# Issuing the sums and normalising of one attention step ahead of the next step's scores

## The chip, the cores and the metric

The kernel runs on one core of a Trainium2 chip. The metric is the device time of one execution in microseconds (us). Before the change it is 1518.8 us, the median of 3 runs (1518.49 to 1519.86). A core has five engines that work side by side, each on its own queue of instructions in order: TensorE (PE: matrix products and transposes), VectorE (DVE), ScalarE (ACT), GpSimd (POOL) and SyncE (SP), which issues most DMAs. An instruction that has to wait holds up everything behind it on its engine.

## The reference

One step of a two-layer network over 384 tokens of width 1024: 128 context tokens and 256 latent tokens. Each layer is SwiGLU, a mixer, SwiGLU, each behind a norm with a shift, a scale and a gate. The mixer of layer 0 ("even") is differential attention with 4 heads beside a short convolution; that of layer 1 ("odd") is attention with 16 query heads, 4 key heads, a window and a sink logit. Context tokens see only context tokens.

```python
# even: two softmaxes per head, subtracted; one query block (128 rows) at a time
s = jnp.einsum("bqhmd,bkhmd->bhmqk", qi, k) * scale
p = jax.nn.softmax(s, axis=-1)
a = p[:, :, 0] - lam * p[:, :, 1]
o = jnp.einsum("bhqk,bkhe->bqhe", a, v)
# odd: one softmax over context keys, latent keys in the window, and a sink
s_l = jnp.where(valid, s_l, -jnp.inf)
p = jax.nn.softmax(jnp.concatenate([s_c, s_l, sink_column], axis=-1), axis=-1)
o = (jnp.einsum("bgrqc,bcgd->bqgrd", p[..., :p_len], v_ctx)
     + jnp.einsum("bgrqk,bkgd->bqgrd", p[..., p_len:-1], vs))
```

## The kernel before

The 384 tokens lie along the free dimension, so a weight block of 128 by 128 meets 384 columns at once. Float32 products are made of three matmuls on split operands (`mm3`, L178 to L180): every weight unit of 1024 x 256 is split into a high part (`wh`, ACT, L80) and a low part (`wl`, L84, in two halves: DVE, and in the mixers GpSimd for the second). `refill` or `refill_half` does the next split at the end of each step of a pipeline. Instructions are issued in the order in which the Python code runs; no scheduler reorders them.

Attention is cut into steps and run by `pipeline`. A step has four parts, of which those of several steps interleave:

- `a`, the scores: PE makes the scores of two maps in two PSUM tiles (`s`), DVE takes their maxima (`mx` L961, `omx` L1221), multiplies by the scale and negates (`ng` L963; `omx` L1223, `ong` L1225, `oes` L1229), ACT takes the exponentials with their row sums (L971; L1233, and L1237 for the sink's term `oes`).
- `m`, the sums, reciprocals and normalising. Even (`combined`): DVE alone, L980 to L992. Odd (`normalised`): an add L1241 and a reciprocal L1242 on two columns on DVE, then one multiply of both maps on GpSimd (L1243).
- `b`, the transposes on PE (`aT`) and their copies by ACT into `at_sb` (L1008, L1255).
- `c`, the products with the values on PE (`o` L1022, `oo` L1266), and at the end of a group of steps what follows it (even: squares, sums and `on`; odd: the split of `oo` into `gh` by ACT L1273 and `gl` by DVE L1274).

At the pipeline's step s, `a` is that of attention step s, `m` that of s-1, `b` that of s-lag and `c` that of s-lag-1. Between `m` and `b` stands `fill`, which gives PE other work: even, the convolution's projections (`conv_chunks`, with their own work on DVE and ACT); odd, pieces of the projections of later queries with their rotary embedding (`rope`, four DVE operations), and near the end the first products of the output projection.

Even has 9 steps and lag 2: step 0 has eight maps of 128 keys for the context tokens, steps 1 to 8 have two maps of 384 keys. Odd has 24 steps and lag 3: every third step (0, 3, 6, ...) is of 128 keys, the others of 384. The scores use the PSUM tag "at" and the transposes "mm", four tiles each, shared with other users.

Of the kernel before, what the change touches and what calls it, by code (L numbers as in the profile page):

```python
# [58 lines left out]
class Weights:  # L59
# [82 lines left out]
    def refill(self):  # L142
        self.split(self.np + self.SPLIT)
# [10 lines left out]
class Kernel:  # L154
# [637 lines left out]
    def pipeline(self, n, a, m, b, c, lag, fill, refill):  # L792

        for s in range(n + lag + 1):
            if s < n:
                a(s)
            if 0 <= s - 1 < n:
                m(s - 1)
            fill(s)
            if 0 <= s - lag < n:  # L800
                b(s - lag)
            if 0 <= s - lag - 1 < n:
                c(s - lag - 1)
            refill()
# [832 lines left out]
```

## Time and profile before

| | |
|---|---|
| median of 3 runs | 1518.8 us |
| the profiled execution's own time | 1518.26 us |
| its span, first to last instruction | 1516.5 us |
| PE busy | 1480.2 us, 98% of the span |
| DVE busy | 1065.0 us, 70% |
| ACT busy | 654.8 us, 43% |
| POOL busy | 147.6 us, 10% |
| chain that ended last: PE, DVE, ACT | 86%, 7%, 2% |
| even attention pipeline | about 383 to 455 us after the span's start |
| odd attention pipeline | about 1106 to 1203 us |

Busy time of an engine counts its instructions, not its waits. The chain that ended last follows the last instruction back to what released it, step by step; a share of PE in it says that PE's own queue set the time there. In the two attention stages an instruction's start, read beside the end of what it needs, says who was late.

### The profile page before, as it was taken

How to read it: one execution, taken by the hardware profiler on the slowest of the kernel's cores; microseconds unless marked ns; L12 is line 12 of the kernel's file. 1: busy time of each engine (PE TensorE's matmuls, PEld its weight loads, DVE VectorE, ACT ScalarE, POOL GpSimd, SP SyncE). 2: the span in 40 equal slices, each digit the busy share in tenths (PEclk: the TensorE clock that was granted, in tenths of full speed). 3: DMA queues.
4: the chain of work that ended last, by engine and by line, in shares of the span. 5: the costliest groups of instructions: out<-in, count | busy, mean ns of one | idle time of the engine just before them, and what ended most of it. 6: DMA issues, size and time to landing. Idle time of an engine off the chain costs nothing.

```text
span 1516.5 us, 22716 instructions
## 1 busy us (share of the span) xinstructions
PE 1480.2 (98%) x9082; PEld 1414.6 (93%) x9082; DVE 1065.0 (70%) x1702; ACT 654.8 (43%) x1203; POOL 147.6 (10%) x99
## 2 busy tenths in 40 slices
PE   6999999999999999999999999999998999999998
PEld 6899999999899999999999999999965799999998
DVE  3848898787777887797779868876786485434442
ACT  4632333465555543233454333324666564223331
POOL 0100000015322100000010000000454220000000
PEclk9999999999999999999999999999998999999999
DMA  9848687633323476676536656743230034433421
GB/s 348 280 155 278 202 262 246 215 117 112 108 88 116 144 232 209 202 237 213 187 105 222 223 180 214 245 165 126 86 100 29 5 112 145 134 117 127 139 91 42
DMA packets 191899, 248.61 MB, mean 164 GB/s; under 512 B 5589, under 2 KB 170034, under 8 KB 191794
## 3 DMA queue, kind: packets, MB, share of 16 engines
q1 hardware_dynamic: 190718, 245.79, 49.1%
q8 instruction: 71, 1.16, 0.3%
q10 hardware_dynamic: 1076, 1.38, 0.3%
q14 instruction: 34, 0.28, 0.1%
HBM read 244.26 MB, written 2.36 MB: 163 GB/s over the span
## 4 chain that ended last, share of the span: by engine, by line
PE 86%; DVE 7%; ACT 2%; issue 2%; POOL 1%; DMA 1%; SPq 0%; ACTq 0%; POOLq 0%; DVEq 0%
PE proj L178 18%; PE proj L180 18%; PE proj L179 18%; PE down L178 9%; PE down L179 9%; PE down L180 8%; DVE wl L84 1%; PE m_sum L237 1%; PE oo L1266 1%; DVE acc L342 1%; PE s L1208 1%; PE aT L1253 1%; DMA wm<-in_w_mod 1%; DVE x L347 1%; ACT wh L80 1%
## 5 line engine op out<-in xcount | busy, mean ns | idle before, releaser
L178 PE MATMUL proj<-xh,wh 128*128 128x384 f32 (+1 forms) x1648 | 563.1, 342 | 3.6 <-ACT bias L518 1.8
L180 PE MATMUL proj<-xh,wl 128*128 128x384 f32 (+1 forms) x1648 | 557.3, 338 | 1.1 <-DVE wl L84 1.1
L179 PE MATMUL proj<-xl,wh 128*128 128x384 f32 (+1 forms) x1648 | 556.3, 338 | 0.0
L84 DVE TENSOR_TENSOR wl<-raw,wh 128x1024 fp32r<-128x1024 f32 (+1 forms) x300 | 357.1, 1229 | 148.6 <-ACT wh L80 148.1
L80 ACT ACTIVATE wh<-raw 128x1024 fp32r<-128x1024 f32 x324 | 317.0, 1027 | 152.7 <-PE down L179 79.7
L178 PEld LDWEIGHTS proj<-xh,wh 128*128 128x128 f32 x1648 | 310.5, 188 | 18.2 <-issue 8.5
L180 PEld LDWEIGHTS proj<-xh,wl 128*128 128x128 f32 x1648 | 311.1, 189 | 1.4 <-DVE wl L84 1.4
L179 PEld LDWEIGHTS proj<-xl,wh 128*128 128x128 f32 x1648 | 310.6, 188 | 0.0
L178 PE MATMUL down<-gh,wh 128*128 128x384 f32 x832 | 280.3, 337 | 0.6 <-ACT gh L634 0.6
L179 PE MATMUL down<-gl,wh 128*128 128x384 f32 x832 | 278.8, 335 | 1.3 <-DVE gl L635 1.3
L180 PE MATMUL down<-gh,wl 128*128 128x384 f32 x832 | 278.3, 334 | 0.0
L225 DVE SCALAR_TENSOR_TENSOR macc<-wm,cpad,macc 128x1024 f32<-128x1024 f32 x210 | 259.1, 1279 | 0.1
L178 PEld LDWEIGHTS down<-gh,wh 128*128 128x128 f32 x832 | 156.3, 188 | 3.4 <-issue 2.3
L179 PEld LDWEIGHTS down<-gl,wh 128*128 128x128 f32 x832 | 156.4, 188 | 2.9 <-DVE gl L635 2.6
L180 PEld LDWEIGHTS down<-gh,wl 128*128 128x128 f32 x832 | 156.3, 188 | 0.0
L634 ACT ACTIVATE gh<-gf 128x768 fp32r<-128x768 f32 x44 | 37.2, 846 | 269.9 <-DVE gf L624 265.4
L347 DVE SCALAR_TENSOR_TENSOR x<-down,m,x 128x128 f32<-128x128 f32 x224 | 82.5, 411 | 72.5 <-PE down L180 72.5
L617 ACT ACTIVATE sg<-proj 128x384 f32<-128x384 f32 x78 | 37.9, 490 | 157.9 <-PE proj L180 157.7
L624 DVE TENSOR_TENSOR gf<-proj,sg 128x384 f32<-128x384 f32 x78 | 43.3, 555 | 79.4 <-PE proj L180 79.4
L84 POOL TENSOR_TENSOR wl<-raw,wh 128x1024 fp32r<-128x1024 f32 x24 | 61.3, 2558 | 107.3 <-ACT wh L80 95.4
L635 DVE TENSOR_TENSOR gl<-gf,gh 128x768 fp32r<-128x768 f32 x44 | 42.2, 959 | 40.1 <-ACT gh L634 40.1
L189 POOL TENSOR_TENSOR nr<-nv,neghalf 128x3 f32<-128x3 f32 x6 | 5.1, 852 | 570.6 <-DVE nv L415 570.6
(221 smaller groups left out, 1083.5 us busy)
## 6 DMA issues: line engine op xcount, KB each, us to landing
raw<-in_ffn_w SPq DMA_DIRECT2D x117, 1024.0 KB
wm<-in_w_mod SPq DMA_DIRECT2D x126, 512.0 KB
raw<-in_ffn_w SPq DMA_DIRECT2D x16, 768.0 KB
raw<-in_even_w_in SPq DMA_DIRECT2D x12, 1024.0 KB
raw<-in_odd_w_in SPq DMA_DIRECT2D x6, 1024.0 KB
raw<-in_even_w_out SPq DMA_DIRECT2D x4, 1024.0 KB
raw<-in_odd_w_out SPq DMA_DIRECT2D x4, 1024.0 KB
raw<-in_ffn_w SPq DMA_DIRECT2D x6, 512.0 KB
```

The lines of the kernel that those rows point to most:

```text
L80: self.k.nc.scalar.activation(parts[0][:, a:b], raw[:, a:b], AF.Copy)
L84: engine.tensor_tensor(out=lo[:, a:b], in0=raw[:, a:b], in1=h[:, a:b].bitcast(F32), op=ALU.subtract)
L178: mm(out, w[0], x[0], start=first, stop=False)
L179: mm(out, w[0], x[1], start=False, stop=False)
L180: mm(out, w[1], x[0], start=False, stop=last)
L225: nc.vector.scalar_tensor_tensor(out=acc, in0=t, scalar=c, in1=acc, op0=ALU.mult, op1=ALU.add)
L237: self.nc.tensor.matmul(ps[32 * j:32 * j + 32, 0:256], c, v[:, j], start=first, stop=last)
L347: self.nc.vector.scalar_tensor_tensor(out=self.x[oc][:, a:b], in0=psum[:, a:b], scalar=gate[:, oc, g:g + 1], in1=self.x[oc][:, a:b], op0=A ...
L617: nc.scalar.activation(sg[c], out[:, 0:T], AF.Silu)
L624: nc.vector.tensor_tensor(out=gf[:, c], in0=out[:, 0:T], in1=sg[c], op=ALU.mult)
L634: nc.scalar.activation(gh[:, at:at + 2], gf, AF.Copy)
L635: nc.vector.tensor_tensor(out=gl[:, at:at + 2], in0=gf, in1=gh[:, at:at + 2].bitcast(F32), op=ALU.subtract)
```

## The change

In `pipeline`, `m(s - 1)` is called ahead of `a(s)` and no longer behind it. Nothing else differs.

```diff
     def pipeline(self, n, a, m, b, c, lag, fill, refill):
 
         for s in range(n + lag + 1):
+            if 0 <= s - 1 < n:
+                m(s - 1)
             if s < n:
                 a(s)
-            if 0 <= s - 1 < n:
-                m(s - 1)
             fill(s)
```

The order of instructions changes on DVE alone; on PE, ACT, POOL and SP it is the same as before. The first place is DVE in the even pipeline, from the maxima of step 0 to those of step 1 (`s` scores, `mx` maxima, `ng` their negated scaled values, `rs` row sums, `c_` the second map's factor, `e` the exponentials):

```order
 L955 TENSOR_REDUCE mx<-s 128x4 x2
 L963 SCALAR_TENSOR_TENSOR ng<-mx,erq 128x8
+L980 RECIPROCAL rs<-rs 128x8
+L982 TENSOR_SCALAR c_3769<-rs,neglam 128x4
+L989 TENSOR_SCALAR e<-e,rs 128x128
+L992 SCALAR_TENSOR_TENSOR e<-e,c_3769 128x128
...
 L961 TENSOR_REDUCE mx<-s 128x1 x2
 L963 SCALAR_TENSOR_TENSOR ng<-mx,erq 128x2
-L980 RECIPROCAL rs<-rs 128x8
```

Step 0's reciprocal, its factor and four pairs of L989 and L992 now stand ahead of the maxima of step 1.

The second is DVE in the even pipeline at step 4, behind the weight split that ends step 3:

```order
 L84 TENSOR_TENSOR wl<-raw,wh 128x1024
+L980 RECIPROCAL rs<-rs 128x2
+L982 TENSOR_SCALAR c_3961<-rs,neglam 128x1
+L989 TENSOR_SCALAR e<-e,rs 128x384
+L992 SCALAR_TENSOR_TENSOR e<-e,c_3961 128x384
 L961 TENSOR_REDUCE mx<-s 128x1 x2
 L963 SCALAR_TENSOR_TENSOR ng<-mx,erq 128x2
-L980 RECIPROCAL rs<-rs 128x2
-L982 TENSOR_SCALAR c_3974<-rs,neglam 128x1
```

The four operations of step 3 moved from behind step 4's maxima to ahead of them.

The third is DVE in the odd pipeline where a group of three steps ends (`oo` attention's product, `gl` its low part, `ors` row sums, `oes` the sink's term, `omx` maxima, `ong` their negated values):

```order
 L1229 TENSOR_TENSOR oes<-ong,negsink 128x2
-L1241 TENSOR_TENSOR ors<-ors,oes 128x2
-L1242 RECIPROCAL ors<-ors 128x2
 L1274 TENSOR_TENSOR gl<-oo,gh 128x384
+L1241 TENSOR_TENSOR ors<-ors,oes 128x2
+L1242 RECIPROCAL ors<-ors 128x2
 L1221 TENSOR_REDUCE omx<-s 128x1 x2
```

The add and the reciprocal that go now stand for the step before; they were behind `oes` and `gl` followed, and now the same pair of the step just issued comes behind `gl`, directly ahead of the next maxima.

## Rows read from the trace of the kernel before

**Rows 1.** The page's first part: busy us, share of the span, instructions.

```profile
PE 1480.2 (98%) x9082; PEld 1414.6 (93%) x9082; DVE 1065.0 (70%) x1702; ACT 654.8 (43%) x1203; POOL 147.6 (10%) x99
```

**Rows 2.** Windows, both attention stages: length, engines' busy us, PEclk, DMA share, GB/s.

```profile
383.00:455.00 72.00, 71.87 (x447) 65.36 (x446) 57.12 (x120) 38.41 (x89) 16.64 (x8) 1.00 0.28 90
1106.00:1203.00 97.00, 87.70 (x615) 59.84 (x613) 61.38 (x204) 59.46 (x191) 42.92 (x30) 0.95 0.11 35
```

**Rows 3.** Timeline, DVE, even: start us, us, instruction, idle time before it.

```profile
390.74 1.02 DVE L961 TENSOR_REDUCE mx<-s 128x1 f32<-128x384 f32 x2 [1.16 <-PE s L943]
...
393.34 0.20 DVE L980 RECIPROCAL rs<-rs 128x8 f32<-128x8 f32 x1 [1.38 <-ACT e L971]
...
395.79 0.35 DVE L992 SCALAR_TENSOR_TENSOR e<-e,c 128x128 f32<-128x128 f32 x1
396.69 1.23 DVE L84 TENSOR_TENSOR wl<-raw,wh 128x1024 fp32r<-128x1024 f32 x1 [0.54 <-ACT wh L80]
...
440.72 0.62 DVE L992 SCALAR_TENSOR_TENSOR e<-e,c 128x384 f32<-128x384 f32 x1
```

**Rows 4.** Timeline, ACT, even: exponentials of steps 1, 2, 4, 8; a copy.

```profile
393.59 0.72 ACT L971 ACTIVATE e<-s,ng,erq 128x384 f32<-128x384 f32 x1
...
400.57 0.67 ACT L971 ACTIVATE e<-s,ng,erq 128x384 f32<-128x384 f32 x1 [2.97 <-PE aT L1006]
...
415.09 0.67 ACT L971 ACTIVATE e<-s,ng,erq 128x384 f32<-128x384 f32 x1 [5.28 <-DVE rs L980]
...
417.30 0.47 ACT L1008 ACTIVATE at_sb<-aT 128x384 f32<-128x384 f32 x1
...
440.07 0.67 ACT L971 ACTIVATE e<-s,ng,erq 128x384 f32<-128x384 f32 x1 [4.78 <-DVE ng L963]
```

**Rows 5.** Timeline, PE, even: products with the values of step 2.

```profile
419.38 0.83 PE L1022 MATMUL o<-v,at_sb 128*128 128x128 f32 x6
```

**Rows 6.** Timeline, POOL: a half split in even, a normalising multiply in odd.

```profile
397.73 2.45 POOL L84 TENSOR_TENSOR wl<-raw,wh 128x1024 fp32r<-128x1024 f32 x1 [8.17 <-ACT wh L80]
...
1117.37 1.47 POOL L1243 TENSOR_TENSOR e<-e,ors 128x768 f32<-128x768 f32 x1 [3.01 <-DVE ors L1242]
```

**Rows 7.** Timeline, DVE, odd: steps 3, 14, 15 and the last add.

```profile
1117.64 1.21 DVE L1223 TENSOR_TENSOR omx<-omx,orq 128x2 f32<-128x2 f32 x1
...
1160.50 1.02 DVE L1221 TENSOR_REDUCE omx<-s 128x1 f32<-128x384 f32 x2 [1.96 <-PE s L1215]
...
1161.76 0.16 DVE L1225 SCALAR_TENSOR_TENSOR ong<-omx,negsink 128x2 f32<-128x2 f32 x1
...
1164.10 0.49 DVE L1221 TENSOR_REDUCE omx<-s 128x1 f32<-128x128 f32 x2 [1.70 <-PE s L1208]
...
1166.89 0.56 DVE L1274 TENSOR_TENSOR gl<-oo,gh 128x384 fp32r<-128x384 f32 x1 [1.45 <-ACT gh L1273]
...
1191.68 0.34 DVE L1241 TENSOR_TENSOR ors<-ors,oes 128x2 f32<-128x2 f32 x1 [1.32 <-ACT oes L1237]
```

**Rows 8.** Timeline, ACT, odd: ends of steps 0, 13, 14, 15 and 23.

```profile
1110.29 0.20 ACT L1237 ACTIVATE oes<-oes 128x2 f32<-128x2 f32 x1
...
1159.44 0.20 ACT L1237 ACTIVATE oes<-oes 128x2 f32<-128x2 f32 x1
...
1162.03 0.67 ACT L1233 ACTIVATE e<-s,ong,orq 128x384 f32<-128x384 f32 x1 [1.64 <-DVE ong L1225]
...
1163.34 0.20 ACT L1237 ACTIVATE oes<-oes 128x2 f32<-128x2 f32 x1
...
1165.07 0.46 ACT L1233 ACTIVATE e<-s,ong,orq 128x128 f32<-128x128 f32 x1 [0.77 <-DVE ong L1225]
...
1165.95 0.19 ACT L1237 ACTIVATE oes<-oes 128x2 f32<-128x2 f32 x1
...
1191.35 0.23 ACT L1237 ACTIVATE oes<-oes 128x2 f32<-128x2 f32 x1
```

**Rows 9.** Windows, odd, the stretch in which the clock falls.

```profile
1158.00:1160.00 2.00, 1.40 (x2) 0.50 (x2) 0.47 (x5) 1.87 (x7) 1.35 (x2) 0.51 0.44 114
```

## The prediction

> **What bounds the kernel now.** I read the page's engine shares first: PE is busy for 1480.2 of 1516.5 us, 98% [rows 1], so an edit on another engine costs nothing until PE has to wait for it. The windows of the two attention stages come next. In even PE has no gap to speak of (71.87 us of 72), while DVE has 15 us of idle time and ACT 34. In odd PE stands for 9.3 of 97 us and no other engine is full (DVE 61.4, ACT 59.5): what sets the time there is a round trip between engines [rows 2]. So I read the timelines of DVE and ACT and ask, for each step s, what the maxima wait for and who waits for the exponentials. Steps are named by their number; m, a, b, c are the pipeline's parts.
>
> **What the order takes away.** No instruction is added or removed. The moved part m of step s-1 waits for the row sums of the exponentials of step s-1 on ACT. Before, the maxima of step s stood ahead of that wait and ran beside those exponentials: in even the first reciprocal came after 1.38 us of idle DVE, with the maxima of step 1 done [rows 3]. Now DVE stands at that wait with the maxima queued behind it, so exponentials, sum, maxima and the next exponentials form one chain with nothing beside it. Where the scores come last (odd's maxima of steps 14 and 15 waited 1.96 and 1.70 us for PE, [rows 7]), m fits into the wait for nothing.
>
> **Odd, the new round trip.** Let A be the start of the add L1241. Add and reciprocal are 0.16 us operations; the first maximum follows 0.3 behind A. From maximum to L1225 takes 1.26 us (1160.50 to 1161.76), from there to ACT 0.27, and from the first exponential to the end of `oes` 1.51 (1162.03 to 1163.54); for 128 keys the last is 1.07 (1165.07 to 1166.14) [rows 7, 8].
>
> A second thing comes with the order. GpSimd's multiply now starts about 0.5 us behind A (an estimate: two 0.16 us operations and a handover like that 0.27), just ahead of L1223. The row of step 3 shows what that does: L1223, 0.16 us like its neighbours, took 1.21 us and ended at 1118.85, as the 1.47 us multiply ended at 1118.84 [rows 6, 7]. A 768-column multiply then ends at A + 1.97 and holds L1223 to there: L1225 starts at A + 2.02 and not at 1.5. Behind a step of 128 keys the multiply has a third of the columns and is gone in time.
>
> Per group of three steps, from A to the end of `oes`: step 1 of the group 0.3 + 1.26 + 0.27 + 1.51 = 3.3; step 2 2.02 + 0.27 + 1.51 = 3.8; step 0 2.02 + 0.27 + 1.07 = 3.4. Between them the add starts 0.1 behind `oes` (1191.58 to 1191.68), twice, and once 1.2 behind, since `gl` comes first (1166.14 to 1167.4 with its tail overlapped) [rows 7, 8]. Together 3.3 + 3.8 + 3.4 + 0.1 + 0.1 + 1.2 = 11.9 us.
>
> Steps 15 to 23 take 28.0 us before (1163.54 to 1191.58, [rows 8]); now three groups, 35.7: +7.7. Step 14 takes 3.9 either way. Steps 1 to 13 take 49.2 before (1110.49 to 1159.64). Now: four groups 47.6, and 1.2 + 3.3 for step 13, 52.1; two DVE halves of weight splits and two of GpSimd come between `oes` and the add: 2 x 1.23, and 2 x about 2.1 (2.45 less what passes unseen) [rows 3, 6]; less 2 x 1.1, since steps 0 and 3 have no `gl` yet. That is 56.6: +7.4. Odd gives +15.1. The products of step 24's fill need PSUM tiles that the exponentials of steps 22 and 23 free, and from there PE's queue is full: the delay passes on whole. Bounds: if GpSimd's lock cost nothing a group would take 10.3, which over 7 2/3 groups takes 12 us off, so +3; with scores that come last at each step, nothing; with the maxima blocked by a half split in four more steps, +8 more. I take 15, since the row of the blocked L1223 is the operation itself.
>
> Of that lock the Trainium skill says in "SBUF — State Buffer", section "Who interferes with whom", that a VectorE instruction with two SBUF inputs and a GpSimd instruction that reads SBUF exclude each other, the later one waiting to the end of the first. The 1.21 us row agrees; by a rule of shared bandwidth instead the group would be nearer 10.3.
>
> **Even.** Step 0 has eight maps, so its m is ten operations; the last ends at 396.1, and only then do the maxima of step 1 start, not at 390.74 [rows 3]. With 1.02 + 0.3 us to ACT, step 1's exponentials start at 397.4 instead of 393.59: +3.8 [rows 4]. The weight split behind them on ACT, and with it DVE's half at 396.69, moves by as much, to 400.5. Step 1's L992 then runs into GpSimd's 2.45 us half and ends at 404.5; step 2's exponentials start at 405.8 instead of 400.57: +5.2. From there DVE has the same work per step, with m ahead of each exponential: 1.3 us, as m of step 7 ran from about the start of step 8's exponentials at 440.07 to 441.34 [rows 3, 4]. The split ahead of step 4 ends some 4.9 late by the same reckoning; with m's 1.3, step 4's exponentials start at 421.3 instead of 415.09: +6.2.
>
> Who waits: the copy of step 2's transposes stands behind them on ACT, 2.2 us after their start before (417.30). It moves along, to 423.3 or a little later, and PE's products with the values, at 419.38 before, wait for it. Only 1.6 us lay between the copy's end at 417.77 and that use, so PE loses what the lag has over 1.6: 4.5 us here [rows 4, 5]. From step 4 to step 8 I add 5.2 us to the lag (an estimate, each part at most the 1.5 us of a pass of exponentials): twice 0.9 where the convolution's `gh` now stands behind exponentials that start after its input is ready, 0.5 for one more lock, 1.5 where m of step 6 waits for a whole pass with no fill on DVE, 1.4 where the squares of the first head group do. Step 8's exponentials then start 11.4 late, not at 440.07 but at 451.5, and PE, 1.6 behind that, ends the stage 10 late. Bounds: 0, if DVE's 15 us of idle time swallow the lag before PE meets it; 12, the lag of step 8's exponentials itself. I take 10, since the slack of 1.6 us is a measured one and the first 3.8 come at once.
>
> No DMA moves in its queue, and with DMA shares of 0.28 and 0.11 in these stages weights that are asked for 10 us later are still early [rows 2].
>
> **Sum.** 10 + 15 = 25 us on the profiled execution's own 1518.3: 1543.3. It lies 0.5 under the median of the runs, so 1544 for a median.
>
> **Rivals.**
> 1. Even hides its part: DVE's idle time takes the lag back before ACT's copies are late. For it: PE's full row and 15 us of slack [rows 2]. Against: the lag starts with 3.8 us at once and the copies share ACT's queue with the exponentials. 1518.8 + 15 = 1534. Chance 0.16.
> 2. The clock falls more often. Before, PE at 1.40 us busy of 2 ran at 0.51 of its clock, the 1.2 GHz level, after it had stood for lack of scores [rows 9]; the odd stage's mean is 0.95 [rows 2]. More standing in both stages would give more such stretches; one of 7 us beside dense matmuls loses 3.5, three or four of them 10 to 14: 1555. Chance 0.12. The Trainium skill ("TensorE: Matmul & The Clock Gate", "Part 1: The HAM clock gate") holds that idleness drops the engine to half rate, which speaks for this rival; row 9 agrees.
> 3. No difference: scores come last in nearly all steps, so m runs in DVE's waits. For it the waits of 1.96 and 1.70 us [rows 7]; against it the last add, which waited 1.32 us for ACT with an idle DVE [rows 7]. 1519. Chance 0.07.
> 4. Faster: with scores last, the earlier m lets GpSimd multiply sooner, its lock falls into DVE's waits and not on L1223 or the rotary products, and PE's transposes come sooner. It is worth part of the 9.3 us that PE stands in odd [rows 2]; a third gives 1516. It decides only if `oes` of step s-1 ends before the scores of step s in most odd steps; of the rows, steps 14 and 15 say yes, and the last add no. Chance 0.05.
>
> **Chances and range.** The forecast, both stages slower, has 0.60, its own range 1534 to 1553. The range over the cases is 1526 to 1558: it takes in rival 1 and most of rival 2, and leaves out rivals 3 and 4 and the ends of the rest, some 0.18. Within 0.2% (3 us, about what can be told from no change here): 0.07 by rival 3. Faster 0.05 by rival 4, slower 0.88 by the rest.
>
> **What would show it.** In odd: L1223 between 0.16 and 1.2 us in two of three steps, the gap from `oes` to the next maximum never under 0.4 us, groups of near 12 us, PE idle of some 25 us in the stage. In even: maxima of step 1 behind ten normalising operations, step 4's exponentials near 421 if the stage starts as before, and PE waiting for `at_sb` at L1022. If PE's busy row in even stays at 72 of 72, that half is wrong; if the odd groups stay under 10 us, the other.

## The result, and the profile after

The changed kernel takes 1543.26 us, the median of 4 runs (1541.44 to 1545.08), against 1519.33 us (1518.49 to 1519.96, 4 runs): a ratio of 1.0158 [1.0142, 1.0173], 24 us slower. The forecast was 1544 us, slower. The profiled execution took 1541.44 us, with a span of 1539.6 us; it reached the even stage 2.24 us earlier than the one of before, so times are compared from each stage's first scores: 383.91 and 1106.83 us before, 381.67 and 1114.27 us after. A step's start is called late by what it has moved against them.

The first part of the page, as [rows 1]:

```profile
PE 1489.2 (97%) x9082; PEld 1417.6 (92%) x9082; DVE 1072.0 (70%) x1702; ACT 655.0 (43%) x1203; POOL 147.7 (10%) x99
```

The instruction counts are the same. PE is busy for 9.0 us more without more work, so part of the time went into matmuls that took longer; the rest went into PE standing still. The windows show where, for both attention stages from the first scores to the end of the last product with the values, and for after three windows of 2 us inside the even stage. Columns: length; busy us of PE, PEld, DVE, ACT, POOL; granted clock; DMA share; GB/s. Of before, the two stretches of [rows 2] with those bounds:

```profile
383.91:455.11 71.20, 71.07 (x435) 64.83 (x434) 57.22 (x120) 38.03 (x88) 16.64 (x8) 1.00 0.28 90
1106.83:1202.98 96.15, 86.85 (x610) 59.24 (x610) 60.58 (x202) 58.63 (x191) 42.92 (x30) 0.95 0.11 35
```

And of after:

```profile
381.67:462.14 80.47, 75.66 (x435) 67.54 (x434) 58.67 (x120) 37.62 (x88) 16.66 (x8) 0.96 0.24 80
1114.27:1226.20 111.93, 93.82 (x610) 62.09 (x609) 66.15 (x201) 59.05 (x191) 42.96 (x30) 0.91 0.09 30
422.00:424.00 2.00, 0.54 (x2) 0.00 (x0) 1.85 (x6) 0.61 (x2) 0.00 (x0) 0.98 0.00 0
424.00:426.00 2.00, 1.80 (x3) 0.73 (x4) 0.56 (x1) 2.00 (x7) 0.00 (x0) 0.50 0.00 0
...
430.00:432.00 2.00, 2.00 (x11) 2.00 (x11) 1.97 (x2) 0.00 (x0) 1.28 (x1) 0.81 0.00 0
```

Even takes 80.47 us where it took 71.20 (+9.3), odd 111.9 where it took 96.15 (+15.7): together 25.0 us. Less the 2.24 us by which even began earlier, that is 22.8 of the 23.2 us between the two profiled executions. In even, of the 9.3 us, 4.7 are standing (4.81 where it was 0.13) and 4.6 are longer busy time: PE is busy for 0.54 of the 2 us from 422, and behind that the granted clock is at 0.50, the 1.2 GHz level, until shortly after 430. In odd PE stands 8.8 us longer (18.1 where it was 9.3) and is busy for 7.0 us more, at a mean clock of 0.91 where it was 0.95.

**Odd, one group.** The timeline of DVE of after where the maxima of steps 17 (384 keys) and 18 (128 keys) stand, each behind the add of the step before it (start, duration, instruction, idle time before it):

```profile
1187.52 0.16 DVE L1241 TENSOR_TENSOR ors<-ors,oes 128x2 f32<-128x2 f32 x1 [1.53 <-ACT oes L1237]
...
1187.79 1.00 DVE L1221 TENSOR_REDUCE omx<-s 128x1 f32<-128x384 f32 x2
1188.83 0.70 DVE L1223 TENSOR_TENSOR omx<-omx,orq 128x2 f32<-128x2 f32 x1
...
1191.45 0.16 DVE L1241 TENSOR_TENSOR ors<-ors,oes 128x2 f32<-128x2 f32 x1 [1.53 <-ACT oes L1237]
...
1191.73 0.47 DVE L1221 TENSOR_REDUCE omx<-s 128x1 f32<-128x128 f32 x2
1192.23 1.24 DVE L1223 TENSOR_TENSOR omx<-omx,orq 128x2 f32<-128x2 f32 x1
```

GpSimd in the same stretch:

```profile
1188.05 1.47 POOL L1243 TENSOR_TENSOR e<-e,ors 128x768 f32<-128x768 f32 x1 [2.79 <-DVE ors L1242]
1191.98 1.47 POOL L1243 TENSOR_TENSOR e<-e,ors 128x768 f32<-128x768 f32 x1 [2.47 <-DVE ors L1242]
```

DVE stands 1.53 us for ACT at both adds; at the maxima behind them no idle time is listed: the scores are there already. Then L1223, on two columns, takes 0.70 and 1.24 us and ends as the multiply ends (1189.53 against 1189.52, 1193.47 against 1193.45). The stage's groups of DVE instructions (count, busy us, mean ns, idle before), first of before, then of after:

```profile
L1221 DVE TENSOR_REDUCE omx<-s 128x1 f32<-128x384 f32 (+1 forms) x48 | 20.2, 462 | 9.9 <-PE s L1208 5.4 <-PE s L1215 4.3
L1223 DVE TENSOR_TENSOR omx<-omx,orq 128x2 f32<-128x2 f32 x24 | 11.1, 463 | 0.9
L1241 DVE TENSOR_TENSOR ors<-ors,oes 128x2 f32<-128x2 f32 x24 | 4.0, 166 | 1.6 <-ACT oes L1237 1.3 <-issue 0.3
```

```profile
L1221 DVE TENSOR_REDUCE omx<-s 128x1 f32<-128x384 f32 (+1 forms) x48 | 19.8, 455 | 0.1
L1223 DVE TENSOR_TENSOR omx<-omx,orq 128x2 f32<-128x2 f32 x24 | 17.6, 733 | 0.9
L1241 DVE TENSOR_TENSOR ors<-ors,oes 128x2 f32<-128x2 f32 x24 | 3.8, 158 | 21.1 <-ACT oes L1237 19.1 <-ACT onk L1177 1.9
```

Both costs stand there. The wait: DVE's idle time has moved from the maxima, which waited 9.9 us for scores before and 0.1 us now, to the adds, which wait 19.1 us for ACT where it was 1.3. The hold behind GpSimd, called the lock from here on as in the prediction: L1223 paid for it before too, and now pays more often.

**Even.** DVE of after, the end of step 0's normalising, then the maxima and the normalising of step 1, against [rows 3]:

```profile
393.55 0.35 DVE L992 SCALAR_TENSOR_TENSOR e<-e,c 128x128 f32<-128x128 f32 x1
393.82 1.01 DVE L961 TENSOR_REDUCE mx<-s 128x1 f32<-128x384 f32 x2
...
399.37 2.23 DVE L989 TENSOR_SCALAR e<-e,rs 128x384 f32<-128x384 f32 x1
401.64 0.62 DVE L992 SCALAR_TENSOR_TENSOR e<-e,c 128x384 f32<-128x384 f32 x1
```

DVE of before at that weight split; GpSimd's half (397.73 to 400.18, [rows 6]) held L963, the scaling of step 2's maxima, which takes 0.16 us when nothing holds it:

```profile
398.88 1.32 DVE L963 SCALAR_TENSOR_TENSOR ng<-mx,erq 128x2 f32<-128x2 f32 x1
...
400.44 0.41 DVE L989 TENSOR_SCALAR e<-e,rs 128x384 f32<-128x384 f32 x1
```

The exponentials of steps 1, 2, 4 and 8 on ACT, against [rows 4] (less 2.24 us for the earlier start):

```profile
395.06 0.67 ACT L971 ACTIVATE e<-s,ng,erq 128x384 f32<-128x384 f32 x1 [3.55 <-DVE ng L963]
...
403.50 0.67 ACT L971 ACTIVATE e<-s,ng,erq 128x384 f32<-128x384 f32 x1 [4.68 <-DVE ng L963]
...
418.50 0.67 ACT L971 ACTIVATE e<-s,ng,erq 128x384 f32<-128x384 f32 x1 [6.11 <-DVE ng L963]
...
448.41 0.67 ACT L971 ACTIVATE e<-s,ng,erq 128x384 f32<-128x384 f32 x1 [6.08 <-DVE ng L963]
```

They are late by 3.7, 5.2, 5.7 and 10.6 us. Between step 4 and step 8 four kinds of rows on DVE have grown, first of before, then of after:

```profile
417.43 0.56 DVE L917 TENSOR_TENSOR gl<-y,gh 128x384 fp32r<-128x384 f32 x1 [0.59 <-ACT gh L916]
...
426.30 1.26 DVE L963 SCALAR_TENSOR_TENSOR ng<-mx,erq 128x2 f32<-128x2 f32 x1
...
433.43 0.69 DVE L1033 TENSOR_REDUCE oss<-osq 128x4 f32<-128x512 f32 x1 [2.12 <-ACT osq L1031]
```

```profile
420.36 0.56 DVE L917 TENSOR_TENSOR gl<-y,gh 128x384 fp32r<-128x384 f32 x1 [1.43 <-ACT gh L916]
...
429.29 2.21 DVE L989 TENSOR_SCALAR e<-e,rs 128x384 f32<-128x384 f32 x1
...
434.77 0.17 DVE L980 RECIPROCAL rs<-rs 128x2 f32<-128x2 f32 x1 [1.48 <-ACT e L971]
...
440.46 0.69 DVE L1033 TENSOR_REDUCE oss<-osq 128x4 f32<-128x512 f32 x1 [3.17 <-ACT osq L1031]
```

PE's waits in the stage, summed (us, times, longest), and its timeline around the longest:

```profile
PE s L943 <- ACT e L971: 1.7, 1, 1.7
PE o L1016 <- ACT at_sb L1008: 1.3, 1, 1.3
PE aT L1006 <- DVE y L915: 1.0, 1, 1.0
PE o L1022 <- ACT at_sb L1008: 0.7, 1, 0.7
```

```profile
420.76 0.94 PE L1022 MATMUL o<-v,at_sb 128*128 128x128 f32 x6 [0.72 <-ACT at_sb L1008]
421.63 0.91 PE L943 MATMUL s<-kt,q 64*128 64x384 f32 x2
424.20 1.64 PE L943 MATMUL s<-kt,q 64*128 64x384 f32 x2 [1.67 <-ACT e L971]
```

PE waits for `at_sb`, 1.3 us at step 0's products (L1016) and 0.72 us at step 2's (L1022), but longest for a free PSUM tile: the second score tile of step 6 waits for step 5's exponentials, since the transposed output `oT` holds the fourth "at" tile. The stretch at half clock follows that wait.

### The profile page after: what moved, and what is told of

The parts are those of the page before. It is cut to its first block, busy times and chain, and to the rows that moved or that the text cites. A ratio compares the mean times of both kernels' runs of the same rounds, so it can differ in the third digit from the quotient of the medians.

```text
span 1539.6 us, 22716 instructions
## 1 busy us (share of the span) xinstructions
PE 1489.2 (97%) x9082; PEld 1417.6 (92%) x9082; DVE 1072.0 (70%) x1702; ACT 655.0 (43%) x1203; POOL 147.7 (10%) x99
## 4 chain that ended last, share of the span: by engine, by line
PE 81%; DVE 9%; ACT 4%; issue 3%; POOL 1%; DMA 1%; ACTq 0%; SPq 0%; DVEq 0%; POOLq 0%
PE proj L178 17%; PE proj L180 17%; PE proj L179 17%; PE down L179 8%; PE down L178 8%; PE down L180 8%; DVE wl L84 2%; ACT e L1233 1%; PE m_sum L237 1%; DVE omx L1221 1%; DVE acc L342 1%; DVE omx L1223 1%; ACT wh L80 1%; POOL wl L84 1%; DMA wm<-in_w_mod 1%
## 5 line engine op out<-in xcount | busy, mean ns | idle before, releaser
L189 POOL TENSOR_TENSOR nr<-nv,neghalf 128x3 f32<-128x3 f32 x6 | 5.1, 852 | 570.4 <-DVE nv L415 570.4
```

## Experiments

Eight kernels ran. Their added lines shift the line numbers: L992 of the kernel that puts step 0 back is L989 here, and with one-input maxima L1228, L1233 and L1238 stand for L1221, for L1223 with L1225, and for L1229. The two with one stage alone, the one with one-input maxima on the new order and the one that puts step 0 back share runs of the kernel before at 1518.16 us (8 runs); the others share runs at 1518.47 us (16 runs).

### The new order in one stage alone

Against the changed kernel:

```diff
+            early = lag == 3        # odd_only; lag == 2 in even_only
-            if 0 <= s - 1 < n:
+            if early and 0 <= s - 1 < n:
                 m(s - 1)
             if s < n:
                 a(s)
+            if not early and 0 <= s - 1 < n:
+                m(s - 1)
```

> The new order in the odd pipeline alone; the even one as before. Theory: the two stages' losses add, and odd's is the larger: in the trace of after, odd's last exponentials end 16.6 us later against the stage's own start. So 14 to 17 us slower than before (about 1534.5), even's timeline as before. Rival, the clock: if the falls of the clock in odd are caused by the delay that even hands on, odd alone costs under 10. Rival, position only: 23 x 0.36 us of add and reciprocal ahead of the maxima, 8 us.

Odd alone: 1534.97 us (1534.52 to 1536.68), ratio 1.0114 [1.0096, 1.0132], +16.8 us; the odd stage takes 112.58 us, the even one 71.2.

> The new order in the even pipeline alone; the odd one as before. Theory: 8 to 10 us slower than before (about 1528.5), half of it PE standing (4.8 us in the trace of after) and half products at half clock after it. Rival, position only: 8 steps x 1.3 us of normalising ahead of the maxima, 10 us, but spread over all steps and with no gap before step 1's maxima. Rival, even hides it: under 2.

Even alone: 1529.19 us (1528.14 to 1531.15), ratio 1.0075 [1.0059, 1.0091], +11.0 us; the even stage takes 80.54 us, the odd one 96.18. Each stage loses its own part, by its length as much as in the change (16.4 and 9.3 us, there 15.7 and 9.3). The two medians' losses sum to 27.8 us, more than the change's 24; the even stage begins at 383.9 us in the profiled execution of before and at 381.7 in that of the change, at about 384 and 386 in these, so a few us of a total don't come from the two stages.

### Odd: maxima with one SBUF input

If the lock is what costs, a form of L1223 and L1225 that has only one tensor input should run beside GpSimd's multiply. The scale and the sink then come in as one scalar per partition, and GpSimd negates the scale beforehand.

```diff
-nc.vector.tensor_tensor(out=mx, in0=mx, in1=scale, op=ALU.mult)
-nc.vector.scalar_tensor_tensor(out=ng, in0=mx, scalar=-1.0,
-    in1=self.negsink[:, h0:h0+2], op0=ALU.mult, op1=ALU.min)
 ...
+for p in range(2):
+    nc.vector.tensor_scalar(out=ng[:, p:p+1], in0=mx[:, p:p+1],
+        scalar1=nscale[:, p:p+1], scalar2=self.negsink[:, h0+p:h0+p+1],
+        op0=ALU.mult, op1=ALU.min)
```

> As the changed kernel, but in odd the two operations behind the maxima (a multiply and a combined one with two SBUF inputs each) are replaced by two of one column each that read one tensor and two per-partition scalars; GpSimd makes the negated scales, three small multiplies more. Theory of the lock: they no longer wait for GpSimd's multiply, a group of three steps falls from 12.1 to about 10.5 us, and the kernel gains 9 to 13 us over the changed one: about 1531. Rival, ACT and PE hold the steps anyway: under 3 us gained.

On the new order: 1524.18 us (1523.75 to 1528.91), ratio 1.0053 [1.0035, 1.0071]: 6.0 us over the kernel before, where the change has 24. The direction was as expected, the gain was larger, some 19 us on the changed kernel where 9 to 13 were expected. The odd stage takes 96.11 us, as before the change. The even stage still loses 9.2 us; the total is less because this execution reached it 3.2 us earlier. DVE of this kernel, a step of 128 keys:

```profile
1188.99 0.47 DVE L1228 TENSOR_REDUCE omx<-s 128x1 f32<-128x128 f32 x2
1189.37 0.45 DVE L1233 TENSOR_SCALAR ong<-omx,norq,negsink 128x1 f32<-128x1 f32 x2
1189.85 0.87 DVE L1238 TENSOR_TENSOR oes<-ong,negsink 128x2 f32<-128x2 f32 x1
```

Its GpSimd:

```profile
1189.24 1.47 POOL L1252 TENSOR_TENSOR e<-e,ors 128x768 f32<-128x768 f32 x1 [2.07 <-DVE ors L1251]
```

The pair of one-input operations runs inside the multiply at full speed. The next operation with two SBUF inputs, `oes`, is now the one held, to 1190.72 us; the multiply ends at 1190.71. It stands behind the value that the exponentials wait for, and in front of a term that ACT takes last.

> The kernel before (old order in both stages) with the one-tensor operations behind odd's maxima. In before, the time from the last maximum to the end of L1225 is 0.39 us in 17 odd steps and longer by 7.3 us in sum in the other 7, each time under a GpSimd instruction. Theory of the lock: these go and the odd stage gets 3 to 7 us shorter: 1512 to 1516, faster than before. Rival, PE sets the pace of odd in the old order: within 1.5 us of before.

On the old order: 1514.65 us (1512.23 to 1515.54, 10 runs), ratio 0.9974 [0.9964, 0.9983]; the odd stage takes 91.40 us. The kernel before paid for the same lock too, 4.75 us. With the lock gone from these operations in both, the new order costs 96.11 - 91.40 = 4.7 us in odd: that is the price of the new order without the lock, which is put down here to the wait; the rest of the difference between the two orders was not taken apart.

### Another place for the sums: two steps back

```diff
+            if 0 <= s - 2 < n:
+                m(s - 2)
             if s < n:
                 a(s)
-            if 0 <= s - 1 < n:
-                m(s - 1)
```

Here the sums stand ahead of the maxima too, but of a step whose exponentials have long ended.

> m of step s-2, not s-1, ahead of the scores and maxima of step s, in both stages. The wait for the exponentials just issued is gone, GpSimd's multiply still starts just ahead of L1223. Theory, lock and wait separate: if the lock is what costs odd its time, odd stays 8 to 16 us long; if it is the wait for the exponentials, odd falls back to within 3 us of before. Even has its moved operations still ahead of the maxima: 4 to 7 us. By the lock 1531 to 1541, by the wait 1523 to 1528.

With the lock: 1537.21 us (1535.77 to 1539.04), ratio 1.0121 [1.0105, 1.0137]. Odd takes 102.44 us: 6.3 more than before with no wait for exponentials, and the multiply beside the maxima: L1223 and L1225 are busy for 19.4 us together, 15.0 before. It came out a little under the 8 to 16 that were expected of the lock. Even takes 84.32 us, 13.1 more and far over the 4 to 7 expected: at lag 2 the transposes of that very step follow at once, and PE waits for them. The total lies in the expected range only because the two misses cancel.

```profile
PE aT L1006 <- DVE e L992: 10.0, 8, 2.7
```

> Even in the old order; in odd m of step s-2 ahead of step s's scores and the one-tensor operations behind the maxima: neither a wait for the exponentials just issued nor the lock on the two operations. Theory: the odd stage is shorter than before's by what before loses to the lock, 3 to 7 us, and 0 to 2 us more, as the add runs where DVE waits for scores: 1510 to 1515. Rival, PE sets the pace: within 1.5 us of before.

Odd two steps back with one-input maxima, even as before the change: 1512.90 us (1510.28 to 1513.71, 6 runs), ratio 0.9962 [0.9950, 0.9973], 5.6 us faster than the kernel before, where the change is 24 slower. The odd stage takes 88.90 us:

```profile
1107.82:1196.72 88.90, 82.53 (x610) 56.52 (x610) 56.76 (x201) 58.29 (x191) 43.59 (x33) 1.00 0.12 38
```

PE stands for 6.4 us and the granted clock is 1.00. So sums ahead of the maxima are no bad order by themselves: it needs sums that are ready, and operations behind the maxima that GpSimd doesn't hold. Most of the gain is the lock's: one-input maxima on the old order take 91.40 us of odd already. That the whole kernel is faster than that one is not shown: their intervals overlap.

### Even: which part of the delay is step 0's

```diff
-            if 0 <= s - 1 < n:
+            if 0 <= s - 1 < n and not (lag == 2 and s == 1):
                 m(s - 1)
             if s < n:
                 a(s)
+            if lag == 2 and s == 1:
+                m(0)
```

> As the changed kernel, but in the even pipeline step 1's maxima stand ahead of step 0's eight-map normalising again; all other steps in the new order. Theory: even's loss starts with the 3.8 us by which step 1's exponentials are late; without them step 4's lag falls from 5.7 to about 2, near the slack of 1.6 us, so even costs 0 to 2 instead of 9, and the whole is about 1534 to 1536. Rival, position only (1.3 us in each step): 7/8 of even's loss stays, 1542.

1540.47 us (1538.95 to 1542.64), ratio 1.0149 [1.0131, 1.0167]: a miss, since most of the loss stayed, nearer to the rival's 1542 than to the 1534 to 1536 expected. The even stage takes 77.09 us, so step 0's ten operations were 3.4 of the 9.3 us. Step 1's exponentials are on time again (9.70 us after the first scores, 9.68 before), but those of step 2 are 1.7 late and those of step 8 7.2. In the first of these losses stands a row of DVE, step 1's normalising under GpSimd's half split:

```profile
400.18 2.25 DVE L992 TENSOR_SCALAR e<-e,rs 128x384 f32<-128x384 f32 x1
```

That is 1.8 us over the usual, but the same half split held L963 before, by 1.2 us. So the longer hold makes only some 0.7 of the 1.7 us; the rest is step 1's four operations themselves, which now stand ahead of step 2's maxima. From there on each step adds to it.

### Even: another PSUM tile for the transposed output

```diff
-self.ps("at", "oT")
+self.ps("mm", "oT")
```

> New order in even alone, and the transposes of the placed head group (oT) take a PSUM tile of tag mm instead of at. In the trace of the even-only kernel PE stands 4.7 us, 1.7 of them where step 6's second score tile waits for step 5's first exponential because oT holds the fourth tile; the clock falls right behind that. Theory: without that wait the clock holds, and even costs 3 to 5 us instead of 9 to 11: about 1522. Rival, PE waits as long at the next place: 1527 to 1529.

The new order in even alone, with `oT` taken from the other four tiles: 1529.55 us (1528.04 to 1530.81), ratio 1.0073 [1.0059, 1.0087], the same as without it: the rival's time, not the 1522 expected. The even stage takes 81.27 us (80.54 without). The wait at the score tile is gone, and others stand in its place:

```profile
PE oT L1054 <- ACT at_sb L1011: 1.8, 2, 1.2
PE o L1019 <- ACT at_sb L1011: 1.3, 1, 1.3
PE aT L1009 <- DVE upad L899: 1.3, 1, 1.3
PE proj L178 <- DVE upad L899: 1.1, 1, 1.1
PE aT L1009 <- DVE y L918: 1.0, 1, 1.0
```

Over the stage PE stands for 6.9 us, with a clock of 0.98:

```profile
384.49:465.76 81.27, 74.38 (x435) 65.96 (x434) 58.60 (x120) 37.38 (x88) 16.65 (x8) 0.98 0.25 84
```

Where PE meets the delay differs, the delay hardly does: step 8's exponentials are 10.1 us late here and 10.6 in the change, and the stages end 10.1 and 9.3 late. This speaks for the chain on DVE and ACT as what sets the end.

## Why the prediction was right

**The sum.** Forecast were +15 for odd and +10 for even; measured in the traces, +15.7 and +9.3. The kernels with one stage alone confirm both as causes, at +16.8 and +11.0.

**Odd's round trip.** The gap from the end of `oes` to the next maximum was forecast as never under 0.4 us; it is about 0.38 us in 10 of 23 steps and 0.31 at the least, where it had been negative in 9. Steps 15 to 23 take 36.18 us (35.7 forecast, 28.04 before), steps 1 to 13 take 57.34 (56.6 forecast, 49.15 before). That is 12.06 us for a group of three, against 11.9. The holds fall as reckoned, on step 2 and step 0 of a group and not behind a step of 128 keys: from the last maximum to the end of L1225 it takes 0.39 us in step 1 of a group, 0.93 in step 2, 1.46 in step 0. Longer are steps 1, 4 and 12, with 1.72, 2.40 and 3.56 us, where GpSimd's half of a weight split lies on these operations. The stage's idle time was forecast as some 25 us of PE; it is 18.1, and 7.0 us of longer busy time stand beside it.

**The lock's weight in odd.** The prediction gave the lock some 12 us of its 15 and the wait 3. Measured without the lock on either side, the order costs 4.7 (96.11 - 91.40), which leaves 11.0 of the 15.7 to the lock that the order adds. The time from the last maximum to the end of L1225, as far as it is over 0.39 us, agrees: it sums to 16.3 us in the change and to 7.3 before, and by the timelines some 11.1 of the one and 2.4 of the other lie beside multiplies, the rest beside halves of weight splits. Wrong was the bound as it was put: a lock that cost nothing was to leave +3, and it leaves 0 (96.11 against 96.15 us). The bound took the lock off the multiplies only and left in 2 x 2.1 us for GpSimd's halves of weight splits. These hold the same two operations (L1223 for 2.17 us in step 4, L1225 for 2.26 in step 12), and with the one-input form that goes too. The kernel before paid its 4.75 us mostly to such halves; of rows like the one of 1.21 us [rows 7] it had three (0.66 to 1.21 us).

**Even's first steps.** Step 1's exponentials were forecast 3.8 us late and are 3.7 late; step 2's 5.2, and are 5.2; step 4's 6.2, and are 5.7, since the split ahead of them ends 4.3 late and not 4.9; step 8's 11.4, and are 10.6. The lock in step 1 took the instruction ahead of the one that was named: L989, a multiply by a scalar, went from 0.41 to 2.23 us, and L992 behind it took its usual 0.62. The time was the same, since the two follow each other in one chain. Of the 1.8 us only some 0.7 are new: before, the same half held L963. The Trainium skill says in "SBUF — State Buffer", "Who interferes with whom", that `tensor_scalar` in a two-port mode excludes GpSimd as well, for the whole instruction. The 2.23 us agree, as L989 ends at 401.60 us and GpSimd's half, which started first, at 401.38. The one-input form on a single column is held nowhere in odd (0.45 us for two, inside a multiply); why it isn't, no run here shows.

**Even's later steps.** From step 4 to step 8 the prediction added 5.2 us to the lag, an estimate in four parts; the lag grows by 4.9. The rows of DVE shown above have each part: the convolution's `gl` waits 0.84 and 0.77 us longer for `gh` (0.9 each were forecast), the hold at the next half split is 0.7 longer (2.21 us at L989 over 0.41, before 1.26 at L963 over 0.16; 0.5 forecast), the reciprocal of step 6 waits 1.48 for its exponentials (1.5), and the sums of squares wait 1.05 longer (1.4). Together that is 4.8. It is read from one trace of each kernel; no run took a single part away.

**Even's place and kind of loss.** Here a step failed: the one by which PE meets the lag in one wait, for `at_sb` at L1022, and loses there what the lag has over 1.6 us, 4.5 us in standing. That wait came, but with 0.7 us. PE was 3.6 us late at these products (39.09 us behind the first scores, 35.47 before), most of it from waits ahead of them, 1.3 us for `at_sb` at step 0's products and 1.0 at transposes. In all PE stands for 4.7 us at four places, the longest at a score tile that the prediction had not looked at, and 4.6 of the 9.3 us are longer busy time. From 424 to 431 us PE is busy for 6.80 us at a granted clock of 0.52, which makes some 3.3 of the 4.6 (an estimate: 6.80 x 0.48): rival 2's mechanism, inside the forecast. The moved `oT` shows that the wait at the score tile is not the cause, since without it the stage is no shorter. That the clock is not the cause either is argued, not shown: it was at 0.98 there and not at 1.00. What the prediction had right is the end. The stage ends 1.3 us less late than step 8's exponentials in the change (9.3 and 10.6) and with step 0 put back (5.9 and 7.2), where 1.6 was reckoned; with the moved `oT` both are 10.1. So the number rests on the chain of DVE and ACT, which was forecast, and not on the wait of PE, which was wrong.

**The rivals.** Even hidden (1534) fell with even alone at +11.0. The lower clock (1555) came in odd too, with a mean of 0.91 and PE busy for 7.0 us more, but a group takes what the round trip alone asks (12.06 against 11.9 us) and the maxima wait for scores for 0.1 us, so it added nothing that can be seen. The prediction misread its row: ahead of the fall of the clock in [rows 9] PE had not stood for lack of scores; its own score products waited 2.06 us for DVE's L702, which reads a PSUM tile of the same tag. No difference and faster fell with the gap of 0.38 us. The condition of the fourth, sums that are ready when the scores are awaited, is the one that two steps back met; with the lock out of the way its odd stage is 2.5 us shorter than that of the old order (88.90 against 91.40, one trace each).

## What to carry to other kernels

An instruction that waits, moved ahead of one that doesn't on the same engine, puts the second behind the wait and makes one chain of two; before moving it, look at which of the two was ready first in most steps. It also moves what it releases on other engines: here a GpSimd multiply came to lie on a two-column operation of DVE, and that cost over twice what the wait did (11.0 against 4.7 us). The same order two steps back, with nothing for GpSimd to hold, made odd shorter. Where PE meets a delay of other engines need not be its cause: here, moving the place only moved the wait.

## What the runs showed of the hardware

The hold of a DVE instruction by GpSimd doesn't go by its size alone. Two columns with two tensor inputs were held for 1.1 us by a multiply (1.24 us where 0.16 is usual), and two operations on one column with scalars took 0.45 us together beside a multiply of the same size. One tensor input is no safety either: the multiply of 384 columns by a scalar took 2.23 us beside a half split and not 0.41. Nor does every GpSimd instruction hold: in the change L1223 took its 0.16 us at 1116.27 while the power on 12 columns (L189) was listed as running from 1114.71 to 1117.89; the profile's times on GpSimd are rough.
